# Weight matrices stored in DRAM in the order and shape in which the kernel loads them

## The chip, the cores and the metric

One core of one Trainium2 chip runs the whole program. The metric is device time in microseconds (us) of one execution, as the median of several runs. The core has TensorE (PE: matmuls, and PEld for its weight loads), VectorE (DVE), ScalarE (ACT), GpSimd (POOL) and SyncE (SP), and 16 DMA engines. SP issues all the DMAs of this kernel; the 16 engines carry them out.

## The reference, cut to what matters

Two blocks in sequence on 256 tokens of 1024 features, in float32:

```
x = first_block(...)     # modulation (w_ada), in projection (w_in), Fourier mix and
                         # neighbourhood attention, gates (w_branch_gate), out projections
                         # (w_fourier_out, w_attn_out, w_out), MLP (w_mlp1, w_mlp2)
second_block(x, ...):
  h = rms_norm_2(x);  p = h @ w_in_2                 # memory attention, conv branch,
  x = x + concat(branches) @ w_out_2                 # two-way recurrent branch
  # 16 experts, each takes its 32 best tokens of 256
  xe  = h[idx]
  hid = silu(xe @ w_gate[e]) * (xe @ w_up[e])        # each weight [1024, 1024]
  ye  = (hid @ w_down[e]) * gates
  x   = x.at[idx].add(ye);  final norm
```

The experts' weights are 16 x 3 matrices of 4 MB, 201 MB together. The other large weights are about 100 MB together.

## The kernel before

The program runs through the stages in the order above. Every weight is read once, in pieces of 1 MB (in a few places 512, 640 or 768 KB), each by one DMA of SP into a place of 128 partitions x 8 KB. The tiles are the same before and after: a piece in SBUF always holds 2048 float32 (8 KB) per partition.

- `wload` (line 273) loads a piece of the first block and of the second block's projections into one of a few places called `raw`. Its source is a view of the weight as `jax` stores it, row after row. SP issues the next load into a place as soon as the last reader of the place is done. `wsplit` (line 282) then makes two tiles `split` from it on ACT and DVE (a high and a low part), and TensorE multiplies these.
- `dense_steps` takes pieces of all 1024 rows and 256 columns (its matrices are w_in_2, w_branch_gate, w_mlp1, w_out and others): partition p gets, from each of eight groups of 128 rows, 256 columns, so eight runs of 1 KB. With 512 rows (w_fourier_out, w_attn_out) there are four runs of 2 KB.
- `tok_steps` takes pieces of 512 rows and 512 columns (w_in): four runs of 2 KB, of rows 8 KB apart in DRAM.
- `first` (w_in, columns 0 to 1023) and `down` (w_mlp2) take 256 rows: two runs of 4 KB.
- `shift_scale` takes the first third of w_ada in eight pieces of 256 columns: eight runs of 1 KB. `ada_steps` takes the other two thirds in 16 pieces of 128 rows and 2048 columns: already one run of 8 KB per partition, of rows 24 KB apart.
- `ring_load` (line 1818) issues the loads of the experts' weights into a ring of places, called `ew`; a load is issued on SP when a place comes free. The order of the pieces is fixed: for each expert four pieces of gate, four of up, four of down. Each is 256 rows of 1024 columns, so two runs of 4 KB per partition. The down matrix of the last expert is loaded by columns (`LAST`, line 32): three pieces of 256 columns (eight runs of 1 KB) and two of 128 columns (eight runs of 512 bytes).

In the expert loop TensorE multiplies the gate and up pieces into `pgu`, ACT and DVE make `hid` of it, TensorE transposes it (`phT`), multiplies the down pieces into `pd`, and adds the gated result into `acc`. The products go through the line 249, for all stages. TensorE works at one of two clocks, 2.4 GHz or 1.2 GHz; the profile shows the granted clock as a share of the higher one.

Of the kernel before, what the change touches and what calls it, by code (L numbers as in the profile page):

```python
# [31 lines left out]
LAST = (0, 256), (512, 768), (256, 384), (768, 1024), (384, 512)  # columns of the last expert's results, in order  # L32
# [97 lines left out]
# ---------------------------------------------------------------- layout of the small inputs  # L130
# [13 lines left out]
_o = 0  # L144
# [36 lines left out]

def arrays(inputs):
    out = {}
    for n in _BIG:
        a = np.ascontiguousarray(np.asarray(inputs[n]))
# [20 lines left out]
class Body:  # L206
# [7 lines left out]
    # ---- small helpers  # L214
# [47 lines left out]
    # ---- weights: loaded in pieces of 1 MB, split in halves of a piece  # L262
# [10 lines left out]
    def wload(self, src, k):  # L273
# [6 lines left out]
        return view  # L280
# [11 lines left out]
    def dense_steps(self, w, c0, c1, nk, sets, evacs, pieces=None, wide=False, preload=0, fine=False, between=None):  # L292
# [10 lines left out]
        def load(c):  # L303
            piece[c] = self.wload(w[0:nk * 128, c:c + per].rearrange("(k p) f -> p k f", p=128), nk)
# [66 lines left out]
    def tok_steps(self, w, c0, c1, sets, outs):  # L371
        """Products of [1024 features] with the tokens out on partitions: outs()[set][half], psum."""
# [5 lines left out]
        def prepare(r, h):  # L378
            if h == 0:
                piece[r] = self.wload(w[r * 128:(r + kc) * 128, c0:c1].rearrange("(k p) f -> p k f", p=128), kc)  # L380
            return self.wsplit(piece[r][:, h * kc // 2:(h + 1) * kc // 2])
# [18 lines left out]
    def in_turn(self, engines="PE DVE Activation"):  # L400
        """What follows comes after what was traced before on these engines."""
# [35 lines left out]
    def rstd(self, ps):  # L437
        """Reciprocal norms along the free axis [128, 256], the same on all partitions, from sums of squares [128, 2]."""
# [7 lines left out]
    def transpose_in(self, tok, out):  # L446
        """Two tiles [128, 1024] with the tokens on partitions to [128, 8, 256] features on partitions."""
# [58 lines left out]
    # ---- the whole  # L506
# [70 lines left out]
    def memory(self, tok, y):  # L577
        """Keys and values of the memory: steps for its norm, the keys, the values.

        tok, y: allocate two tiles [128, 1024], one [128, 16, 256]."""  # L580
# [24 lines left out]
        return (self.normed(A["mem_2"], tok, mT),  # L605
                [(None, scale)] + self.dense_steps(A["w_mk_2"], 0, 256, 8, H, [ev]),
                self.tok_steps(A["w_mv_2"], 0, 256, H, outs) + [(None, out)])

    def ada_steps(self, bank, mod, tag="pw"):
        """A third of the modulation: mod[:, r, i] for its 16 feature tiles."""  # L610
        w = self.A["w_ada"]
        acc = {}

        def prepare(k):
            return self.wload(w[k * 128:(k + 1) * 128, bank * 2048:(bank + 1) * 2048]
                              .rearrange("p (k f) -> p k f", k=4), 4)
# [39 lines left out]
    def mixers(self, x0):  # L656
        tc, nc, A, sm = self.tc, self.nc, self.A, self.sm
        w = A["w_in"]
# [26 lines left out]
        with ExitStack() as es:  # L685
# [20 lines left out]
            def shift_scale(g):  # L706
                """The first third of the modulation for the feature tiles 2 g, 2 g + 1, and their inputs."""
                bank, raws = {}, []

                def load(z):  # L710
                    c = z * 1024 + g * 256
                    raws.append(self.wload(A["w_ada"][:, c:c + 256].rearrange("(k p) f -> p k f", p=128), 8))
# [29 lines left out]
            def first():  # L742
                """Fourier features and queries, eight feature tiles side by side for inputs that come one by one."""
# [3 lines left out]
                def load(n):  # L747
                    piece[n] = self.wload(w[n * 256:(n + 1) * 256, 0:1024].rearrange("(k p) f -> p k f", p=128), 2)
# [27 lines left out]
            def weave(steps, others, n):  # L776
                """One of the others after each n of the steps."""
# [50 lines left out]
        with att as es:  # L828
# [8 lines left out]
            def norms(_):  # L837
                """Reciprocal norms of q, k and context k."""
# [31 lines left out]
            def score(i, e, j):  # L870
                """Softmax of 128 queries of a head."""
# [20 lines left out]
            def apply(i, e, j):  # L892
                """The values of the same queries."""
# [45 lines left out]
            def gating():  # L939
                for z in range(2):  # L940
# [4 lines left out]
                    yield from self.dense_steps(A["w_branch_gate"], z * 1024, (z + 1) * 1024, 8, [X], [ev_g])  # L945

            def out_fourier():
# [3 lines left out]
                return self.dense_steps(A["w_fourier_out"], 0, 1024, 4, [(yfh, yfl)], [ev])  # L951
# [28 lines left out]
    def merge_mlp(self, x0, yfh, yfl, yah, yal, gates):  # L980
        nc, A, b8 = self.nc, self.A, self.b8
        modB, modC = self.mod[1], self.mod[2]
        with ExitStack() as es:
# [41 lines left out]
            # MLP  # L1025
# [4 lines left out]
            def up(c):  # L1030
# [8 lines left out]
                return self.dense_steps(A["w_mlp1"], c * 256, (c + 1) * 256, 8, H, [ev_u], wide=c == 0)  # L1039

            def down(c):
                piece = []

                def prepare(k):
                    if k == 0:
                        piece.append(self.wload(A["w_mlp2"][c * 256:(c + 1) * 256, :]
                                                .rearrange("(k p) f -> p k f", p=128), 2))
# [18 lines left out]
            def down_last():  # L1066
                """The last three halves of pieces side by side, so that the sums end one after the other."""
# [29 lines left out]
            def steps():  # L1097
                ao = self.dense_steps(A["w_attn_out"], 0, 1024, 4, [(yah, yal)], [ev_a])
                wo = self.dense_steps(A["w_out"], 0, 1024, 8, [(mhi, mlo)], [ev_o], wide=True)
# [23 lines left out]
    def block2(self, x2):  # L1123
        """Adds the three branches to x2."""
        with ExitStack() as es:
# [5 lines left out]
            # the branches' results, (hi, lo) per feature tile  # L1131
# [23 lines left out]
    def out_proj(self, x, ob, h, between=0):  # L1155
        """Part of the rows of the out projection, added to x."""
        def ev(i, pv):
# [3 lines left out]
        return self.dense_steps(self.A["w_out_2"][a * 128:b * 128], 0, 1024, b - a, [o], [ev], preload=2, fine=not h,  # L1161
                                between=between and partial(self.ring_load, between))

    def branches(self, x2, hi, lo, ob):
        tc, nc, A, sm, rp = self.tc, self.nc, self.A, self.sm, self.rp
        w = A["w_in_2"]
        # small weights and constants
# [5 lines left out]
        def matrices(n):  # L1173
            """Room for masked scores, which serves the projections before."""
# [22 lines left out]
        # ---- projections  # L1197
# [42 lines left out]
        # ---- memory attention  # L1240
# [54 lines left out]
        def decays():  # L1295
            """Learning rates, decays and gates from the narrow projections."""
# [53 lines left out]
        def keys():  # L1350
# [5 lines left out]
            # reciprocal norms of the heads, on the rows 32 i, 32 i + 1  # L1356
# [18 lines left out]
        def start(d):  # L1375
            """Decayed keys and queries."""
# [49 lines left out]
        # ---- conv branch  # L1426
# [3 lines left out]
        def conv_pe():  # L1430
            """Taps of the last tile: products on ScalarE, summed by TensorE."""
# [43 lines left out]
        # ---- recurrent branch  # L1475
# [6 lines left out]
        # what lasts longest first  # L1482
# [11 lines left out]
        def pad(d, i):  # L1494
            """Queries of two heads, each with zeros for the other, [f, e, j, y, t]."""
# [4 lines left out]
        def scores(d, i, z):  # L1500
            """Masked scores of two heads and both chunks, [s, y, (chunk, head), t]."""
# [12 lines left out]
        def diagonal(d, i):  # L1514
            """The diagonal blocks of 16."""
# [8 lines left out]
        def values(d, i):  # L1524
            """Token-major keys of the first chunk; the values through the scores of the keys."""
# [19 lines left out]
        def first_scores(d):  # L1545
            """What the inverses need."""
# [14 lines left out]
        def blocks16(d):  # L1561
            """Inverses of the diagonal blocks of 16, rows on partitions; then as block-diagonal matrices."""
# [580 lines left out]
```

## Time and profile before

| | |
|---|---|
| time, median of 3 runs | 1208.2 us (1208.07 to 1209.84) |
| span of the profiled execution | 1205.4 us |
| what lies around that span, by the median | 2.8 us |
| busy PE / DVE / ACT | 1078.5 / 513.1 / 431.8 us |
| bytes moved by DMA | 313.89 MB, in 127687 packets |

The span runs from the first to the last instruction of the profiled execution; the runs are timed without the profiler, so the two differ. A packet is one contiguous run that a DMA engine moves. The DMA share of a stretch is the time of its packets summed over the 16 engines, over 16 times the stretch; it can pass 100% because one packet's time overlaps its neighbour's a little. GB/s is what the 16 engines moved together. A busy PE includes matmuls that are slowed by a low clock.

### The profile page before, as it was taken

The page shows a single profiled execution, that of the slowest core. Times are in us where ns is not written, and L with a number is a line of the kernel's source. Part 1 is how long each engine was busy: PE and PEld are TensorE (multiplying, and loading weights), DVE is VectorE, ACT ScalarE, POOL GpSimd, SP SyncE. Part 2 cuts the span into 40 slices and gives each one's busy share as a digit, 9 for nine tenths or more (in the row PEclk, how much of TensorE's full clock was granted, in tenths as well). Part 3 has the DMA queues.
Part 4 walks back from the last instruction along what each step waited for, and adds up shares of the span by engine and source line. Part 5 has one row for each costly group of instructions (what it writes and reads, how often), then busy time and mean ns, then how long its engine had stood idle before and what let it go on. Part 6 is the DMA issues. An engine that isn't in the chain of part 4 may idle for free.

```text
span 1205.4 us, 19234 instructions
## 1 busy us (share of the span) xinstructions
PE 1078.5 (89%) x8140; PEld 759.2 (63%) x8140; DVE 513.1 (43%) x968; ACT 431.8 (36%) x742; POOL 47.6 (4%) x53
## 2 busy tenths in 40 slices
PE   4999999999999999998899998999777777777785
PEld 3886677899999999998578786435322222222222
DVE  2554355577655555669896554212111111111102
ACT  3541367657444444575654433111000000000003
POOL 0010000011000000102210002000000000000000
PEclk8999999999999999999999998999978888888886
DMA  9874545574665563431101478999999999999997
GB/s 325 306 258 174 175 137 196 184 245 148 213 199 175 179 196 125 163 106 39 68 1 58 151 282 346 400 408 409 409 408 409 409 408 409 408 409 409 409 409 252
DMA packets 127687, 313.89 MB, mean 260 GB/s; under 512 B 6128, under 2 KB 65776, under 8 KB 125424
## 3 DMA queue, kind: packets, MB, share of 16 engines
q1 hardware_dynamic: 127600, 312.66, 70.4%
q8 instruction: 64, 1.05, 0.4%
q14 instruction: 23, 0.19, 0.0%
HBM read 311.59 MB, written 1.05 MB: 259 GB/s over the span
## 4 chain that ended last, share of the span: by engine, by line
PE 70%; DMA 20%; DVE 5%; ACT 2%; issue 1%; POOL 1%; SPq 1%; ACTq 0%; DVEq 0%
PE pw L249 23%; DMA ew<-in_w_e_up_dram 18%; PE pd L249 9%; PE acc L249 9%; PE pgu L249 5%; PE pv L249 2%; PE pada L249 2%; PE pqf L249 2%; PE py L249 1%; PE pg L249 1%; PE psc L249 1%; PE po L249 1%; DMA raw<-in_w_ada_dram 1%; PE pp L249 1%; PE psab L249 1%; DMA ew<-in_w_e_down_dram 1%
## 5 line engine op out<-in xcount | busy, mean ns | idle before, releaser
L234 DVE TENSOR_TENSOR split<-raw,split 128x1024 fp32r<-128x1024 f32 (+2 forms) x148 | 176.7, 1204 | 115.0 <-ACT split L228 114.4
L249 PE MATMUL pgu<-ew,XE 128*32 128x256 f32 x2048 | 150.9, 431 | 59.6 <-DMA ew<-in_w_e_up_dram 54.6
L228 ACT ACTIVATE split<-raw 128x1024 fp32r<-128x1024 f32 (+2 forms) x148 | 151.5, 1032 | 123.8 <-PE pw L249 63.0
L249 PE MATMUL pd<-ew,hidT 128*32 128x512 f32 (+2 forms) x560 | 159.7, 619 | 9.1 <-DVE hidT L2037 7.7
L249 PEld LDWEIGHTS pgu<-ew,XE 128*32 128x32 f32 x2048 | 64.6, 119 | 136.3 <-DMA ew<-in_w_e_up_dram 81.4
L249 PEld LDWEIGHTS pd<-ew,hidT 128*32 128x32 f32 x560 | 42.0, 120 | 116.9 <-issue 101.4
L249 PE MATMUL acc<-uh,split 128*128 128x256 f32 x512 | 94.7, 283 | 0.0
L249 PE MATMUL pw<-h2h,split 128*128 128x256 f32 x512 | 92.9, 280 | 0.0
L246 DVE SCALAR_TENSOR_TENSOR hid<-pgu,rs,hid 128x256 f32<-128x256 f32 x16 | 7.7, 484 | 197.3 <-ACT hid L225 197.3
L246 DVE SCALAR_TENSOR_TENSOR ye<-pd,ig,ye 128x512 fp32r<-128x512 f32 (+2 forms) x35 | 24.6, 705 | 151.2 <-ACT ye L225 149.6
L225 ACT ACTIVATE hid<-pgu,rs 128x256 f32<-128x256 f32 x16 | 7.6, 474 | 222.7 <-PE pgu L249 222.7
L225 ACT ACTIVATE ye<-pd,ig 128x512 fp32r<-128x512 f32 (+2 forms) x35 | 22.8, 651 | 173.6 <-PE pd L249 173.6
L249 PEld LDWEIGHTS acc<-uh,split 128*128 128x128 f32 x512 | 80.8, 192 | 0.0
L249 PEld LDWEIGHTS pw<-h2h,split 128*128 128x128 f32 x512 | 79.2, 188 | 0.0
L249 PE MATMUL acc<-ul,split 128*128 128x256 f32 x256 | 72.5, 283 | 0.0
L249 PE MATMUL pw<-h2l,split 128*128 128x256 f32 x256 | 71.4, 279 | 0.0
L249 PE MATMUL pw<-hxh,split 128*128 128x256 f32 x320 | 61.5, 286 | 0.0
L249 PE MATMUL pw<-hmh,split 128*128 128x256 f32 x320 | 61.1, 288 | 0.0
L249 PEld LDWEIGHTS pw<-hxh,split 128*128 128x128 f32 x320 | 49.9, 188 | 8.6 <-issue 4.3
L249 PEld LDWEIGHTS pw<-hmh,split 128*128 128x128 f32 x320 | 50.6, 192 | 1.6 <-PE pz L249 0.5
L249 PEld LDWEIGHTS acc<-ul,split 128*128 128x128 f32 x256 | 49.0, 191 | 0.2 <-DVE ul L234 0.2
L249 PEld LDWEIGHTS pw<-h2l,split 128*128 128x128 f32 x256 | 48.0, 187 | 0.0
(444 smaller groups left out, 1789.3 us busy)
## 6 DMA issues: line engine op xcount, KB each, us to landing
ew<-in_w_e_gate_dram SPq DMA_DIRECT2D x64, 1024.0 KB, 18.4
ew<-in_w_e_up_dram SPq DMA_DIRECT2D x64, 1024.0 KB, 18.4
ew<-in_w_e_down_dram SPq DMA_DIRECT2D x63, 1024.0 KB, 18.6
raw<-in_w_mlp_dram SPq DMA_DIRECT2D x32, 1024.0 KB, 5.5
raw<-in_w_ada_dram SPq DMA_DIRECT2D x24, 1024.0 KB, 5.9
raw<-in_w_in_dram SPq DMA_DIRECT2D x18, 1024.0 KB, 5.3
raw<-in_w_branch_gate_dram SPq DMA_DIRECT2D x8, 1024.0 KB, 5.6
raw<-in_w_out_dram SPq DMA_DIRECT2D x4, 1024.0 KB, 7.0
```

What stands on the lines that cost most here:

```text
L225: self.nc.scalar.activation(out, in_, func, **kw)
L228: self.nc.scalar.activation(out, in_, AF.Copy)
L234: self.nc.vector.tensor_tensor(out=out, in0=a, in1=b, op=op)
L246: self.nc.vector.scalar_tensor_tensor(out=out, in0=a, scalar=s, in1=b, op0=op0, op1=op1)
L249: self.nc.tensor.matmul(out, lhsT, rhs, start=start, stop=stop, **kw)
```

## The change

On the host, before the kernel runs, each large weight is stored piece by piece in the order in which the kernel loads it, and within a piece partition after partition: the 8 KB that one partition receives stand together. A piece of 1 MB is then one contiguous block of DRAM, and its DMA has one run of 8 KB per partition. The smaller pieces have runs of 4 KB (the two last ones of 512 KB), 5 KB and 6 KB (the out projection of the second block). The order of the DMAs, their number, their bytes, their destinations, the tiles and every instruction of the compute engines are the same. The pieces of `ada_steps` keep their length of run; their rows are now 8 KB apart and not 24 KB. The small inputs (tokens, constants, masks) are stored as before.

```diff
+_PIECES = {
+    "w_ada": ([(0, 1024, z * 1024 + g * 256, z * 1024 + (g + 1) * 256) for g in range(4) for z in range(2)]
+              + _by_rows(0, 1024, 128, 2048, 4096) + _by_rows(0, 1024, 128, 4096, 6144)),
+    "w_in": (_by_rows(0, 1024, 256, 0, 1024) + _by_cols(0, 1024, 1024, 1536, 256)
+             + _by_rows(0, 1024, 512, 1536, 2048)),
+    "w_branch_gate": _by_cols(0, 1024, 0, 2048, 256),
...
+    "w_mlp1": _by_cols(0, 1024, 0, 4096, 256),
+    "w_mlp2": _by_rows(0, 4096, 256, 0, 1024),
...
+    "w_e_gate_2": _by_rows(0, 16384, 256, 0, 1024),
+    "w_e_up_2": _by_rows(0, 16384, 256, 0, 1024),
+    "w_e_down_2": _by_rows(0, 15360, 256, 0, 1024) + [(15360, 16384, a, b) for a, b in LAST],
+}
...
+def _in_pieces(name, a):
+    a = np.asarray(a)
+    a = a.reshape(-1, a.shape[-1])
+    out = np.empty(a.size, a.dtype)
+    for r0, r1, c0, c1 in _PIECES[name]:
+        o, f = _PLACES[name, r0, r1, c0, c1], c1 - c0
+        out[o:o + (r1 - r0) * f] = a[r0:r1, c0:c1].reshape(-1, 128, f).transpose(1, 0, 2).reshape(-1)
+    return out
...
+    def wsrc(self, name, r0, r1, c0, c1):
+
+        o, n = _PLACES[name, r0, r1, c0, c1], (r1 - r0) * (c1 - c0)
+        return self.A[name][o:o + n].rearrange("(p f) -> p f", p=128)
+
+    def wload(self, name, r0, r1, c0, c1, k=None):
...
-        view = raw[:, 0:k * src.shape[2]].rearrange("p (k f) -> p k f", k=k)
+        src = self.wsrc(name, r0, r1, c0, c1)
+        view = raw[:, 0:src.shape[1]]
...
-            w = self.A[nm][e]
+            flat = t.rearrange("p k f -> p (k f)")
             if (nm, e) == ("w_e_down_2", 15):
                 a, b = LAST[q]
-                t = t.rearrange("p k f -> p (k f)")[:, 0:8 * (b - a)].rearrange("p (k f) -> p k f", k=8)
-                w = w[:, a:b]
+                flat = flat[:, 0:8 * (b - a)]
+                t = flat.rearrange("p (k f) -> p k f", k=8)
+                w = self.wsrc(nm, e * 1024, (e + 1) * 1024, a, b)
             else:
-                w = w[q * 256:(q + 1) * 256]
+                r = e * 1024 + q * 256
+                w = self.wsrc(nm, r, r + 256, 0, 1024)
             with self.in_turn("SP"):
-                self.nc.sync.dma_start(t, w.rearrange("(k p) f -> p k f", p=128))
+                self.nc.sync.dma_start(flat, w)
```

## Rows read from the trace of the kernel before

**Rows 1.** The page: DMA share in tenths and GB/s, 40 slices of 30 us

```profile
DMA  9874545574665563431101478999999999999997
GB/s 325 306 258 174 175 137 196 184 245 148 213 199 175 179 196 125 163 106 39 68 1 58 151 282 346 400 408 409 409 408 409 409 408 409 408 409 409 409 409 252
```

**Rows 2.** The critical chain from 770 us: start, length (us), what

```profile
774.73 6.62 PE pgu L249 x116
...
795.48 6.62 PE pgu L249 x116
...
855.72 18.46 DMA ew<-in_w_e_up_dram
...
906.24 1.98 PE pgu L249 x16
...
967.67 1.98 PE pgu L249 x16
...
1184.04 10.79 DMA ew<-in_w_e_down_dram
```

**Rows 3.** DMA in the stretch 860 to 1180 us: packets, bytes, share of 16 engines

```profile
DMA packets 33999, 130.78 MB, mean 409 GB/s; under 512 B 1994, under 2 KB 2157, under 8 KB 33982
...
q1 hardware_dynamic: 33982, 130.53, 102.3%
...
ew<-in_w_e_up_dram SPq DMA_DIRECT2D x40, 1024.0 KB, 18.6
```

**Rows 4.** DMA from 740 to 765 us, GB/s in slices of 0.6 us

```profile
GB/s 419 400 400 419 406 393 406 419 413 419 374 52 52 26 0 0 59 85 400 419 426 400 406 419 400 393 151 308 406 374 354 413 413 433 387 400 406 419 413 420
```

**Rows 5.** DMA from 17 to 21 us, where only runs of 1 KB are loaded

```profile
DMA packets 1377, 1.39 MB, mean 348 GB/s; under 512 B 16, under 2 KB 1377, under 8 KB 1377
```

**Rows 6.** DMA at 72 to 73.5 and 158 to 159.6 us: w_ada, 8 KB runs alone

```profile
DMA packets 78, 0.64 MB, mean 426 GB/s; under 512 B 0, under 2 KB 0, under 8 KB 0
...
DMA packets 84, 0.69 MB, mean 430 GB/s; under 512 B 0, under 2 KB 0, under 8 KB 0
```

**Rows 7.** DMA at 65.3 to 67 us: 4 KB runs alone, as short a stretch

```profile
DMA packets 190, 0.71 MB, mean 419 GB/s; under 512 B 16, under 2 KB 16, under 8 KB 190
```

**Rows 8.** Windows of 860 to 950 us: busy PE, PEld, DVE, ACT, POOL; clock; DMA

```profile
860.00:900.00 40.00, 29.61 (x256) 11.62 (x256) 4.74 (x11) 1.87 (x4) 0.00 (x0) 0.86 1.03 409
900.00:950.00 50.00, 38.52 (x246) 12.53 (x248) 4.11 (x9) 2.32 (x4) 0.00 (x0) 0.74 1.02 409
```

**Rows 9.** Timeline of PE at the end: start, length, what [idle before, its releaser]

```profile
1188.46 3.66 PE L249 MATMUL pd<-ew,hidT 128*32 128x256 f32 x32 [0.52 <-DVE hidT L2037]
...
1194.97 1.07 PE L249 MATMUL pd<-ew,hidT 128*32 128x256 f32 x16 [0.78 <-DMA ew<-in_w_e_down_dram]
```

**Rows 10.** Timeline of PE at the start, the same columns

```profile
20.59 1.07 PE L249 MATMUL pada<-raw,cs 128*32 128x256 f32 x16 [1.65 <-DVE hxl L234]
23.48 1.94 PE L249 MATMUL pada<-raw,cs 128*32 128x256 f32 x16 [1.82 <-DMA raw<-in_w_ada_dram]
```

**Rows 11.** Windows at the start, columns as in rows 8

```profile
20.00:22.00 2.00, 1.07 (x16) 0.50 (x16) 1.44 (x4) 2.00 (x4) 0.00 (x0) 0.91 1.10 357
22.00:24.00 2.00, 0.52 (x8) 0.29 (x12) 1.87 (x2) 0.42 (x1) 0.00 (x0) 0.50 1.04 404
...
28.00:30.00 2.00, 2.00 (x18) 2.00 (x16) 0.00 (x0) 0.00 (x0) 0.00 (x0) 0.88 1.10 350
```

**Rows 12.** Critical chain, 60 to 720 us: its only DMA

```profile
131.08 5.37 DMA raw<-in_w_branch_gate_dram
```

**Rows 13.** DMA issues from 104 to 112 us: a w_ada load, us to landing

```profile
raw<-in_w_ada_dram SPq DMA_DIRECT2D x1, 1024.0 KB, 4.8
```

**Rows 14.** Waits of 60 to 240 us that end with a DMA: us, times, longest

```profile
ACT split L228 <- DMA raw<-in_w_branch_gate_dram: 7.9, 3, 3.3
...
ACT split L228 <- DMA raw<-in_w_in_dram: 1.1, 1, 1.1
```

**Rows 15.** DMA at 91 to 92.6 and 222.5 to 225 us: 2 KB runs

```profile
DMA packets 297, 0.61 MB, mean 379 GB/s; under 512 B 1, under 2 KB 1, under 8 KB 297
...
DMA packets 512, 1.02 MB, mean 406 GB/s; under 512 B 16, under 2 KB 16, under 8 KB 512
```

More of the change, by code (lines that the diff above doesn't have):

```diff
@@ L179, with _by_rows, _by_cols @@
         "iclr_up_2", "gate_up_2", "w_out_2", "w_router_2", "w_e_gate_2", "w_e_up_2", "w_e_down_2"]
+def _by_rows(r0, r1, n, c0, c1):
+    return [(r, r + n, c0, c1) for r in range(r0, r1, n)]
+def _by_cols(r0, r1, c0, c1, n):
+    return [(r0, r1, c, c + n) for c in range(c0, c1, n)]
+_PIECES = {
[4 more added lines that the diff above has]
+    "w_branch_gate": _by_cols(0, 1024, 0, 2048, 256),
+    "w_fourier_out": _by_cols(0, 512, 0, 1024, 512),
+    "w_attn_out": _by_cols(0, 512, 0, 1024, 512),
+    "w_out": _by_cols(0, 1024, 0, 1024, 256),
+    "w_mlp1": _by_cols(0, 1024, 0, 4096, 256),
+    "w_mlp2": _by_rows(0, 4096, 256, 0, 1024),
+    "w_mk_2": [(0, 1024, 0, 256)],
+    "w_mv_2": [(0, 1024, 0, 256)],
+    "w_in_2": _by_cols(0, 1024, 0, 2560, 256),
+    "w_out_2": _by_cols(0, 640, 0, 1024, 256) + _by_cols(640, 1024, 0, 1024, 512),
+    "w_e_gate_2": _by_rows(0, 16384, 256, 0, 1024),
+    "w_e_up_2": _by_rows(0, 16384, 256, 0, 1024),
+    "w_e_down_2": _by_rows(0, 15360, 256, 0, 1024) + [(15360, 16384, a, b) for a, b in LAST],
+}
+_PLACES = {}
+for _n, _l in _PIECES.items():
+    _o = 0
+    for _p in _l:
+        _PLACES[(_n, *_p)] = _o
+        _o += (_p[1] - _p[0]) * (_p[3] - _p[2])
+def _in_pieces(name, a):
[6 more added lines that the diff above has]
+    return out
 def arrays(inputs):
@@ L184, in arrays @@
     for n in _BIG:
+        if n in _PIECES:
+            out[n] = _in_pieces(n, inputs[n])
+            continue
         a = np.ascontiguousarray(np.asarray(inputs[n]))
@@ L290, in wsplit, with dense_steps @@
         return hi, lo
-    def dense_steps(self, w, c0, c1, nk, sets, evacs, pieces=None, wide=False, preload=0, fine=False, between=None):
+    def dense_steps(self, w, c0, c1, nk, sets, evacs, pieces=None, wide=False, preload=0, fine=False, between=None,
+                    r0=0):
         half = {3: 256, 5: 128}.get(nk) or 1024 // nk
@@ L303, in load @@
         def load(c):
-            piece[c] = self.wload(w[0:nk * 128, c:c + per].rearrange("(k p) f -> p k f", p=128), nk)
+            piece[c] = self.wload(w, r0, r0 + nk * 128, c, c + per)
         def prepare(c, h):
@@ L379, in prepare @@
             if h == 0:
-                piece[r] = self.wload(w[r * 128:(r + kc) * 128, c0:c1].rearrange("(k p) f -> p k f", p=128), kc)
+                piece[r] = self.wload(w, r * 128, (r + kc) * 128, c0, c1)
             return self.wsplit(piece[r][:, h * kc // 2:(h + 1) * kc // 2])
@@ L605, in memory @@
         return (self.normed(A["mem_2"], tok, mT),
-                [(None, scale)] + self.dense_steps(A["w_mk_2"], 0, 256, 8, H, [ev]),
-                self.tok_steps(A["w_mv_2"], 0, 256, H, outs) + [(None, out)])
+                [(None, scale)] + self.dense_steps("w_mk_2", 0, 256, 8, H, [ev]),
+                self.tok_steps("w_mv_2", 0, 256, H, outs) + [(None, out)])
     def ada_steps(self, bank, mod, tag="pw"):
-        w = self.A["w_ada"]
         acc = {}
         def prepare(k):
-            return self.wload(w[k * 128:(k + 1) * 128, bank * 2048:(bank + 1) * 2048]
-                              .rearrange("p (k f) -> p k f", k=4), 4)
+            return self.wload("w_ada", k * 128, (k + 1) * 128, bank * 2048, (bank + 1) * 2048, 4)
         def compute(k, raw):
@@ L657, in mixers @@
         tc, nc, A, sm = self.tc, self.nc, self.A, self.sm
-        w = A["w_in"]
+        w = "w_in"
         both = self.b1.tile([128, 16, 256], F32, tag="y", name="xncn", bufs=1)
@@ L711, in load @@
                     c = z * 1024 + g * 256
-                    raws.append(self.wload(A["w_ada"][:, c:c + 256].rearrange("(k p) f -> p k f", p=128), 8))
+                    raws.append(self.wload("w_ada", 0, 1024, c, c + 256))
                 def products(z):
@@ L747, in load @@
                 def load(n):
-                    piece[n] = self.wload(w[n * 256:(n + 1) * 256, 0:1024].rearrange("(k p) f -> p k f", p=128), 2)
+                    piece[n] = self.wload(w, n * 256, (n + 1) * 256, 0, 1024)
                 def split(k):
@@ L944, in ev_g @@
                         self.act(gates[z][:, i:i + 2], pv, AF.Sigmoid)
-                    yield from self.dense_steps(A["w_branch_gate"], z * 1024, (z + 1) * 1024, 8, [X], [ev_g])
+                    yield from self.dense_steps("w_branch_gate", z * 1024, (z + 1) * 1024, 8, [X], [ev_g])
             def out_fourier():
@@ L950, in ev @@
                     self.tt(g[:, i:i + 2], g[:, i:i + 2], pv, ALU.mult)
-                return self.dense_steps(A["w_fourier_out"], 0, 1024, 4, [(yfh, yfl)], [ev])
+                return self.dense_steps("w_fourier_out", 0, 1024, 4, [(yfh, yfl)], [ev])
             units = [(i, e, j) for i in range(4) for e in range(2) for j in range(2)]
@@ L1038, in ev_u @@
                     self.put_split(uh, ul, r)
-                return self.dense_steps(A["w_mlp1"], c * 256, (c + 1) * 256, 8, H, [ev_u], wide=c == 0)
+                return self.dense_steps("w_mlp1", c * 256, (c + 1) * 256, 8, H, [ev_u], wide=c == 0)
             def down(c):
@@ L1160, in out_proj @@
         o = tuple(Tiles(lambda k, z=z: ob[a + k][:, z]) for z in range(2))
-        return self.dense_steps(self.A["w_out_2"][a * 128:b * 128], 0, 1024, b - a, [o], [ev], preload=2, fine=not h,
-                                between=between and partial(self.ring_load, between))
+        return self.dense_steps("w_out_2", 0, 1024, b - a, [o], [ev], preload=2, fine=not h,
+                                between=between and partial(self.ring_load, between), r0=a * 128)
     def branches(self, x2, hi, lo, ob):
         tc, nc, A, sm, rp = self.tc, self.nc, self.A, self.sm, self.rp
-        w = A["w_in_2"]
+        w = "w_in_2"
         heads = rp.tile([128, 416], F32, name="heads")
```

10 lines of the change are left out of this document (4 added, 6 removed).

## The prediction, before the result was known

> **What bounds the kernel now.** I read the page's slices first: the DMA rate stands at 408 to 409 GB/s, flat, from slice 27 to slice 39, and far below it in the middle of the kernel [rows 1]. A flat ceiling over 13 slices, with the share of the DMA engines in the highest tenth, is what a transfer bound looks like. The chain of waits says from when it decides. Until 841 us an expert follows the one before in 20.7 us (774.73 to 795.48) and the chain holds TensorE alone; from 855 us each round holds a wait of some 18 to 22 us for an up piece, and two rounds take 61.4 us (906.24 to 967.67), 30.7 us per expert [rows 2]. An expert is 12 pieces of 1 MB, 12.58 MB; at 409 GB/s that is 30.8 us, the same number. So TensorE can do an expert in 20.7 us and gets one in 30.7 us. The windows agree: with 409 GB/s, TensorE is busy 30 of 40 us, part of them at the lower clock (granted share 0.74 to 0.86), so it has room [rows 8]. A piece needs 18.6 us from issue to landing [rows 3], which at 409 GB/s is seven pieces in the queue: the DMA engines never wait for an issue there.
>
> From when is the queue full? At 746 to 751 us the rate falls to zero once, because no place of the ring is free; from 751 us it stays [rows 4]. Between 751 and 855 us TensorE sets the chain, but it works off pieces that have landed and frees places faster (12.58 MB in 20.7 us, 608 GB/s) than the engines fill them. The stream therefore runs without a break from 751 us to the landing of the last up piece at 1184.04 us [rows 2, 4]: 433 us whose length is bytes over rate.
>
> In the rest DMA stands on the chain in two places: a load of w_ada at the start, for which TensorE sits idle 1.82 us [rows 10], and one load of w_branch_gate at 131 us [rows 12]. In the MLP and in the second block the pieces arrive before TensorE wants them.
>
> **The change, part by part.** No instruction of a compute engine is added or removed, and the bytes are the same. What changes is the number of packets: a 1 MB piece of an expert has 128 and not 256, a piece of `dense_steps` 128 and not 1024. So the question is what a packet costs beside its bytes.
>
> *The stream of experts.* Runs of 1 KB, with the queue full, come at 348 GB/s [rows 5], runs of 4 KB at 409 [rows 3]. Per engine that is 16 x 1.024/348 = 47.1 ns and 16 x 4.096/409 = 160.2 ns a packet: 37.7 ns for each KB and 9.4 ns for the packet. By that line a packet of 8 KB takes 311 ns, or 421.5 GB/s. The trace holds runs of 8 KB too, in the loads of w_ada: in two short stretches with nothing else they came at 426 and 430 GB/s [rows 6]. Short stretches flatter: 4 KB runs reach 419 in one [rows 7] where the long stream has 409. I take the line. 433 us x (1 - 409/421.5) = **12.8 us**. Bounds: from stretch to stretch (419 to 428) the gain is 2.1%, 9.1 us; if the long stream reached the 430 of the best stretch, 433 x (1 - 409/430) = 21.1 us; if it keeps 409, nothing.
>
> *The end.* The last down matrix comes in runs of 1 KB and 512 B. In the profile 4 MB of it need 10.79 us after the last up piece [rows 2]; at 421 GB/s they need 10.0 us, and the smaller packets' cost that is saved belongs to the part ahead too. But TensorE begins on them only at 1188.46 and waits for one of them 0.78 us [rows 9]. All other steps from the last up piece to the end are products, gates and the norm. So the end gives **0.8 us**, bounds 0 and 0.8.
>
> *The start.* The awaited w_ada load is the fourth of its kind, behind one w_in piece and behind the tokens. Four pieces at 348 GB/s take 3.01 us each, at 421.5 GB/s 2.49: 2.1 us sooner, and the w_in piece a little. That covers the wait of 1.82 us. TensorE's clock is at half there: it fell within 20 to 22 us, about when the product before the wait ended, and came back shortly after 28 us [rows 10, 11]. If that stretch keeps its place, work done earlier in it runs at half speed and the 1.82 us bring **0.9 us**. Bounds: nothing (another wait takes its place: DVE's `split`, which must end first) and 1.8 us (the clock does not fall).
>
> *The load at 131 us.* It is alone in the queue, 5.37 us from issue to landing [rows 12]. A lone load with 8 KB runs takes 4.8 us [rows 13]. ACT waits for it at the end, so **0.4 us** of the 0.6 pass on; ACT's two other waits of its kind [rows 14] are off the chain. Bounds 0 and 1.0, should the others count.
>
> *SP's issues* are as many and in the same order; SP waits for places, not for its own work. I cost this at nothing. Where loads are hidden (MLP, second block) they land sooner and TensorE does not see it; nothing hangs on that cover, since landing sooner uncovers no work.
>
> Sum: 12.8 + 0.8 + 0.9 + 0.4 = 14.9 us. The profiled execution has a span of 1205.4 us, so the new span is 1190.5; the runs' median is 2.8 us above the span, and I carry that over: 1208.2 - 14.9 = **1193.3 us**, a ratio of 0.988.
>
> **The rivals.**
>
> *The packet's own cost is smaller in a long stream than the line says.* For: the shortest stretches differ less, 419 against 426 GB/s [rows 6, 7], or 1.6%. Against: over several us 1 KB runs lie 15% under 4 KB runs, which needs a cost of about 9 ns for each packet. The stage then gives 433 x 0.016 = 7.1 us, and with the 2.1 us of the other parts the time is 1199.0.
> The Trainium skill, page "DMA: Bandwidth & Descriptors", section "Why small descriptors are slow (HBM only)", gives a packet a fixed overhead of about 3 cycles beside one per 32 bytes; by that a run of 8 KB costs 259 cycles for twice 131, an estimate of 1.1% or 5.0 us for the stage, and 1201.1 us in all. The trace speaks against so small a price: by the same rule 1 KB runs would lie 6% under 4 KB runs, and they lie 15% under [rows 3, 5].
>
> *Nothing in the long stream.* Something other than the packets sets 409 GB/s (the memory, the way into SBUF), or the 8 KB are moved as two packets again. For: the rate is very flat [rows 1], and flatter than in the short stretches. Against: w_ada's rows show packets of 8 KB above 420 [rows 6]. Then only 2.1 us are left: 1206.1, within the measurement.
>
> *Slower: the new addresses collide.* In step, the 16 engines now read blocks whose partitions lie 8 KB apart, all pieces alike. For: one load whose rows lie 8 KB apart, of 2 KB runs, came at 379 GB/s, where 2 KB runs at 4 KB distance came at 406 [rows 15]; the stretch is short and includes a start. Against: the expert pieces of before are read at distances that are powers of two as well (4 KB), at 409. If the stream fell to 379, the stage would take 433 x (409/379 - 1) = 34 us more: 1240. It decides from below 407 GB/s on, where the stage loses what the other parts bring.
> [...]
>
> *The stream reaches the rate of the best stretch*, 430 GB/s [rows 6]: 21.1 + 2.1 us, 1185.0.
>
> **How the numbers follow.** Chances: forecast 0.72 (its own range 1188 to 1198); smaller packet cost 0.08; nothing in the stream 0.07; slower 0.06; best rate 0.07. The range of 8 in 10 takes in the smaller packet cost on one side and half of the best rate on the other: 1186 to 1202. About 0.2%, 2.4 us, is what a measurement can tell from no change here. Forecast, smaller cost and best rate are faster by more: 0.87; nothing in the stream, 2.1 us, counts as the same: 0.07; the collision is slower: 0.06.
>
> **What would show it.** In the profile after: packets of the main queue fall to less than half, with most of 8 KB; the flat part of the DMA row stands near 421 GB/s; two experts take 59.7 us and not 61.4; the chain still has the up pieces, a little shorter. At the end TensorE no longer waits for a down piece; at the start the 1.82 us before `pada` are gone; loads that were 1 KB runs show up to 420 GB/s. Wrong would be: a flat part at 409 with packets of 8 KB (the bytes are the limit), a rate with dips (collisions), or a flat part at 421 with gaps in which the engines wait for a free place, since then the ring and not the rate would set the length.

## The result, and the profile after

The changed kernel takes 1191.6 us (median of 4 runs, 1191.05 to 1192.07), before 1208.2 (1208.07 to 1209.84): a ratio of 0.9865, with an interval of 0.9851 to 0.9879. It is faster by 16.7 us; predicted were 14.9. Its profiled execution has a span of 1189.8 us against 1205.4, which is 15.6 us less. In all runs of this case that have both on record the time lies 1.7 to 1.9 us above the span. The 2.8 us of before therefore say that its profile is of an execution about 1 us shorter than the median: the stretches below can show 15.6 of the 16.7 us.

The page of the changed kernel, answering to [rows 1]: DMA share and GB/s in 40 slices, all packets, and the main queue.

```profile
DMA  9774545464555543521101368899999999999996
GB/s 357 291 275 155 177 155 194 182 240 146 212 195 191 177 178 111 207 108 36 72 1 46 142 269 358 355 419 420 418 421 418 420 419 418 420 419 421 418 420 273
DMA packets 46919, 313.89 MB, mean 264 GB/s; under 512 B 6128, under 2 KB 6896, under 8 KB 10480
...
q1 hardware_dynamic: 46832, 312.66, 66.6%
```

The bytes are those of before, the packets 46919 instead of 127687, and the flat part of the rate stands at 418 to 421 GB/s.

DMA of the changed kernel from 860 to 1160 us, answering to [rows 3], with the time from issue to landing as the last number:

```profile
DMA packets 17260, 125.80 MB, mean 419 GB/s; under 512 B 1918, under 2 KB 1918, under 8 KB 1918
...
q1 hardware_dynamic: 17244, 125.56, 101.0%
...
ew<-in_w_e_up_dram SPq DMA_DIRECT2D x40, 1024.0 KB, 19.9
```

All but the 1918 small packets now have 8 KB. The engines are as full as before and move 2.5% more. The chain of the changed kernel, answering to [rows 2] (start, length, work):

```profile
899.30 1.98 PE pgu L299 x16
...
919.26 19.92 DMA ew<-in_w_e_down_dram
...
939.24 19.88 DMA ew<-in_w_e_up_dram
...
959.19 19.89 DMA ew<-in_w_e_gate_dram
...
1080.37 1.98 PE pgu L299 x16
...
1160.22 19.11 DMA ew<-in_w_e_down_dram
```

The stretch is still bound by transfers. From 899.30 to 1080.37 us six experts pass, 60.4 us for two. New is that a transfer on the chain often follows a transfer, with no product between them; the last section says why.

To place the gain I cut each span at three points that every kernel has: the first product into `pss`, the first into `pxe` (the tokens of an expert, ahead of the stream; its start on the chain), and the start of the last product with an up piece (the last group of `pgu`). In us:

| profile | to `pss` | to `pxe` | to the last up product | to the end | GB/s, 860 to 1160 us |
|---|---|---|---|---|---|
| before | 57.6 | 687.9 | 438.7 | 21.2 | 409 |
| changed | 54.6 | 687.6 | 428.4 | 19.2 | 419 |
| difference | -3.0 | -0.3 | -10.3 | -2.0 | |

### The profile page after: what moved, and what is told of

Its sections match the earlier page's. It is cut to its first block, busy times and chain, and to the rows that moved or that the text cites. A ratio compares the mean times of both kernels' runs of the same rounds, so it can differ in the third digit from the quotient of the medians.

```text
span 1189.8 us, 19234 instructions
## 1 busy us (share of the span) xinstructions
PE 1074.5 (90%) x8140; PEld 758.5 (64%) x8140; DVE 513.0 (43%) x968; ACT 431.9 (36%) x742; POOL 47.6 (4%) x53
## 2 busy tenths in 40 slices
DMA packets 46919, 313.89 MB, mean 264 GB/s; under 512 B 6128, under 2 KB 6896, under 8 KB 10480
## 4 chain that ended last, share of the span: by engine, by line
PE 62%; DMA 31%; DVE 2%; ACT 2%; POOL 1%; issue 1%; SPq 0%; ACTq 0%
PE pw L299 23%; DMA ew<-in_w_e_down_dram 12%; DMA ew<-in_w_e_up_dram 11%; PE acc L299 8%; DMA ew<-in_w_e_gate_dram 7%; PE pd L299 4%; PE pada L299 2%; PE pv L299 2%; PE psab L299 2%; PE pqf L299 2%; PE pgu L299 2%; PE py L299 1%; PE pg L299 1%; PE psc L299 1%; PE po L299 1%; DMA raw<-in_w_ada_dram 1%
## 5 line engine op out<-in xcount | busy, mean ns | idle before, releaser
L299 PE MATMUL pd<-ew,hidT 128*32 128x512 f32 (+2 forms) x560 | 156.9, 603 | 9.5 <-DVE hidT L2093 7.8
## 6 DMA issues: line engine op xcount, KB each, us to landing
ew<-in_w_e_gate_dram SPq DMA_DIRECT2D x64, 1024.0 KB, 19.9
ew<-in_w_e_up_dram SPq DMA_DIRECT2D x64, 1024.0 KB, 19.9
ew<-in_w_e_down_dram SPq DMA_DIRECT2D x63, 1024.0 KB, 19.9
```

Source lines behind the costliest of these rows:

```text
L299: self.nc.tensor.matmul(out, lhsT, rhs, start=start, stop=stop, **kw)
```

## The experiments

Each kernel is the changed one with the edit shown. Times are medians; ratios are to the kernel before on the same chip, with their 95% intervals. The stretches are those of the table above and come from one execution each; that of all but experts is the longest of its five (1204.9 us), so its stretches show 2.4 of the 5.1 us that the median gives.

| run | us | ratio | to `pss` | to `pxe` | to last up | end | GB/s |
|---|---|---|---|---|---|---|---|
| experts only | 1195.1 | 0.9884 to 0.9914 | 58.2 | 688.1 | 427.0 | 19.7 | 419 |
| all but experts | 1202.4 | 0.9945 to 0.9973 | 57.2 | 687.2 | 437.4 | 21.2 | 409 |
| w_ada only | 1207.1 | 0.9984 to 1.0002 | 56.3 | 687.8 | 438.7 | 22.9 | 409 |
| w_ada and w_in only | 1205.0 | 0.9967 to 0.9985 | 55.4 | 688.2 | 438.4 | 21.2 | 409 |
| the others only | 1206.2 | 0.9974 to 0.9993 | 57.3 | 687.7 | 438.6 | 21.2 | 409 |
| experts, 8 KB runs 32 KB apart | 1192.7 | 0.9864 to 0.9894 | 54.8 | 689.4 | 428.1 | 19.1 | 419 |
| experts, 2 KB runs | 1228.7 | 1.0158 to 1.0188 | 54.9 | 687.4 | 463.8 | 20.3 | 386 |
| experts, 1 KB runs (one run) | 1276.1 | | 54.7 | 687.3 | 512.6 | 19.9 | 348 |
| last matrix in short runs | 1194.7 | 0.9872 to 0.9904 | 56.3 | 687.9 | 427.4 | 21.1 | 419 |
| experts, two pieces by a load | 1196.9 | 0.9899 to 0.9926 | 54.6 | 687.7 | 433.2 | 19.8 | 424 |
| changed, once more | 1189.9 | 0.9841 to 0.9880 | 54.2 | 687.2 | 427.2 | 19.2 | 419 |

**Halves of the change.** A weight that stays as it was stored is sent unchanged and read by rows:

```diff
+        if _plain(name):
+            return self.A[name][r0:r1, c0:c1].rearrange("(k p) f -> p k f", p=128)
```

`_plain` is true for all but the experts' weights (first run), for those alone (second), for all but w_ada (third).

> Only the experts' three weights are stored in pieces; all other weights as in the kernel before. Theory, that each packet costs some 8 to 9 ns of an engine's time beside its bytes: the stream of experts runs at 419 GB/s as in the changed kernel and is 10.0 us shorter, the end is 2.2 us shorter, the start is as before: 1208.2 - 12.2 = 1196.0 us, packets of the main queue about 79000. Rival, that the first part's shorter loads feed the stream (an earlier start of it is where the time comes from): 1203 us or more, and 409 GB/s.

> The reverse of the run before: all weights but the experts' are stored in pieces. Theory: the stream stays at 409 GB/s and only starts sooner, by 3.3 us, of which 2.9 us arise before 30 us: 1204.9 us. Rival, that the gain outside the stream is the one wait of 1.82 us and the load at 131 us as forecast (0.9 + 0.4 us): 1206.9 us. A sum of this gain and that of the experts alone that lies well off 16.7 us would mean that the two parts work on each other.

> Only w_ada is stored in pieces. Theory, that TensorE waits at the start twice for loads of w_ada (at 20.59 us too, where the profile names DVE): the third load's product begins at about 18.8 us and not at 20.6, the fourth at 21.2 and not 23.5, and the time falls by 2.9 us to 1205.3 us. Rival, that the first of the two waits was DVE's hxl as the profile names it, and went away for another reason (the w_in pieces, SP's blocked issues): the third product still begins at 20.6 us and the time is 1207 us.

The experts alone bring 12.4 us (1207.5 to 1195.1), the rest 5.1: together 17.5, about what the whole brings (16.7, and 17.5 in its second measurement). The halves add up, and the rest gave more than the 3.3 us expected of it. The third run missed: 0.4 us, with an interval that holds no change, where 2.9 were expected. Its timeline of PE shows why (start, length, work, idle time before and what ended it):

```profile
19.32 1.07 PE L307 MATMUL pada<-raw,cs 128*32 128x256 f32 x16
...
21.30 1.07 PE L307 MATMUL pada<-raw,cs 128*32 128x256 f32 x16 [0.91 <-DMA raw<-in_w_ada_dram]
...
41.66 1.07 PE L307 MATMUL pada<-raw,cs 128*32 128x256 f32 x16 [2.11 <-DMA raw<-in_w_ada_dram]
```

The first products came about as early as expected (19.32 and 21.30, expected 18.8 and 21.2), but a later load of w_ada, in a queue with w_in pieces that are still stored by rows, kept TensorE waiting 2.11 us at 41.66. The end of this execution took 22.9 us, its last products at the lower clock. So two more runs part the rest in two:

> w_ada and w_in are stored in pieces, nothing else. With w_ada alone the time fell by 0.4 us (not told from nothing), with all weights but the experts' by 5.1. Theory, that the start needs both, since pieces of both stand in the same queue and a faster w_ada only moves the wait to a later piece behind a w_in piece (at 41 us TensorE waited 2.1 us for a w_ada load in that run): 3 to 5 us less than the kernel before, 1202.5 to 1204.5 us beside its 1207.5. Rival, that the start gives nothing and the others of the first part do it: within 1 us of the kernel before.

> The complement: the weights of the gates, of the out projections, of the MLP and of the second block are stored in pieces; w_ada, w_in and the experts' as before. Theory: only the load of w_branch_gate at 131 us stood on the chain, so 0.3 to 0.5 us less than the kernel before, which is inside the interval: ratio 0.9990 to 1.0000. Rival, that these weights hold the rest of the 5.1 us: 1203 to 1205 us.

w_ada with w_in gives 2.8 us, a little under the 3 to 5 expected, and the others 1.5 by the medians and 2.0 by the ratio, more than the 0.3 to 0.5 expected. So the start needs w_in beside w_ada; that w_in pieces ahead in the queue are the reason is argued and not shown. The profile of the others shows only 0.3 us at the start and 0.2 in the middle; about 1 us of it has no place in the trace and stays open.

**Where the runs lie.** The first run below spreads a piece's 8 KB runs over an expert's matrix, 32 KB apart:

```diff
+    if name.startswith("w_e_"):
+        m = (15 if name == "w_e_down_2" else 16) * 1024 * 1024
+        out[:m] = out[:m].reshape(-1, 4, 128, 2048).transpose(0, 2, 1, 3).reshape(-1)
...
```

The second keeps a piece as one block of 1 MB, but stores it as 4 blocks of [128, 512], so that a partition gets four runs of 2 KB; a third does the same with 8, runs of 1 KB:

```diff
+def _runs(name, r0, r1, c0, c1):
+    return 4 if name.startswith("w_e_") and r1 - r0 == 256 else 1
...
+        x = a[r0:r1, c0:c1].reshape(-1, 128, f).transpose(1, 0, 2).reshape(128, n, -1)
+        out[o:o + (r1 - r0) * f] = x.transpose(1, 0, 2).reshape(-1)
```

> The changed kernel, but the four pieces of each expert's matrix are interleaved in DRAM: still one run of 8 KB per partition, but the runs of one piece lie 32 KB apart and not 8 KB, and no piece is one block. Theory, that the number of packets alone counts: no change from the changed kernel, 1191.6 us, 419 GB/s, the same packets. Rival, that the contiguous block of 1 MB or the distance of the runs sets the rate: between 1193 and 1208 us, with the flat part between 409 and 418 GB/s.

> The changed kernel, but each full piece of the experts' weights is stored as four blocks of 128 x 2 KB: the piece is still one contiguous block of 1 MB, loaded in the same order, with four runs of 2 KB per partition. Theory, a fixed cost per packet: from 4 KB (409 GB/s, 160.2 ns of an engine a packet) and 8 KB (419, 312.8 ns) follow 7.6 ns for the packet and 38.15 ns for each KB, so 83.9 ns for 2 KB and 391 GB/s; the stream of 177 MB takes 453 us and not 423: about 1222 us. With the forecast's line (9.4 ns and 37.7 ns) it would be 386 GB/s and 1227 us. Rival, that the contiguous block is what counts: 419 GB/s and 1192 us.

> As the run with 2 KB, with eight blocks of 128 x 1 KB per piece. Runs of 2 KB came at 386 GB/s, 84.9 ns a packet. Theory, a fixed cost per packet: 47.1 ns and 348 GB/s as in the stretch of w_ada loads at the start of the kernel before; the stream of 177 MB takes 508 us, the time is about 1277 us. Rival, that the low rate at the start came from the distance of w_ada's rows or from the start itself: over 360 GB/s and under 1260 us.

DMA from 860 to 1160 us, in this order: runs 32 KB apart, 2 KB runs, 1 KB runs.

```profile
DMA packets 17256, 125.80 MB, mean 419 GB/s; under 512 B 1914, under 2 KB 1914, under 8 KB 1914
```

```profile
DMA packets 58272, 115.91 MB, mean 386 GB/s; under 512 B 1770, under 2 KB 1770, under 8 KB 58258
...
ew<-in_w_e_up_dram SPq DMA_DIRECT2D x39, 1024.0 KB, 14.4
```

```profile
DMA packets 103205, 104.25 MB, mean 348 GB/s; under 512 B 1588, under 2 KB 103191, under 8 KB 103191
...
ew<-in_w_e_gate_dram SPq DMA_DIRECT2D x36, 1024.0 KB, 11.9
```

8 KB runs out of four interleaved pieces come at the same 419 GB/s. One solid block of 1 MB, in runs of 2 KB, comes at 386, below the 409 of before. So it is neither the block nor, at 8 KB and 32 KB, the distance of the runs; it is their length. The times follow the prediction's line: 2 KB took 1228.7 us where the line gave 1227 (and the later one, from 4 and 8 KB, 1222), 1 KB 1276.1 where 1277 was expected.

**The last matrix** in eight runs per partition again, all else as changed: `_runs` gives 8 for the pieces of `LAST` and 1 elsewhere.

> The changed kernel, but the five pieces of the last expert's down matrix keep their short runs: eight runs of 1 KB (of 512 bytes in the two halves) per partition. Theory, that the end is bound by these loads: the last lands 10.8 us after the last up piece and not 8.7, and the time is 2.0 us above the changed kernel's, 1193.6 us. Forecast's view, that TensorE's own work sets the end but for 0.78 us: 0.8 us above at most, 1192.4 us.

By time this run decides nothing: 0.9872 to 0.9904 overlaps the changed kernel's interval. Its profile, with those of the others, does decide; the section after this one reads them.

**Longer runs than the change has.** Places of 16 KB per partition, each loaded with two pieces by one DMA; single pieces keep 8 KB runs.

```diff
-        self.ring_room(RING0)
+        self.ring_room(RING0, 4)
...
-                w = self.wsrc(nm, r, r + 256, 0, 1024)
+                w = self.A[nm][e * 1048576 + q // 2 * 524288:][:524288].rearrange("(p f) -> p f", p=128)
```

> The changed kernel with 14 of the ring's 21 places joined to seven places of 16 KB per partition: where such a place is free, two pieces that follow each other are loaded by one DMA with one run of 16 KB per partition. Theory, a cost of 7.6 to 9.4 ns for each packet: a packet of 16 KB takes some 618 ns of an engine, 424 GB/s; with two thirds of the pieces in pairs the flat part stands at 422 to 423 GB/s and the time is 3 to 4 us under the changed kernel's on the same chip. Rival, that 419 GB/s is a ceiling of another kind (runs of 8 KB came at 426 and 430 in short stretches but never for long): 419 GB/s and no gain. Second rival: places that come free only after two pieces make the engines wait, and the time is above the changed kernel's.

> The changed kernel once more, beside the run with pairs on one chip: 1191 to 1193 us, ratio to the kernel before 0.985 to 0.988.

DMA from 860 to 1160 us with pairs:

```profile
DMA packets 11329, 127.32 MB, mean 424 GB/s; under 512 B 1253, under 2 KB 1253, under 8 KB 1253
...
q1 hardware_dynamic: 11313, 127.08, 100.5%
```

DMA from 742 to 790 us in slices of 1.2 us, with pairs and then in the changed kernel's second measurement (1189.9 us, a little under the 1191 to 1193 expected):

```profile
GB/s 423 410 416 82 7 0 232 314 437 437 396 259 396 410 410 423 437 437 437 437 423 437 423 246 14 0 14 130 266 430 430 416 485 437 437 423 437 423 437 437
```

```profile
GB/s 41 27 55 266 423 314 348 369 335 410 410 444 403 423 416 437 423 437 410 423 403 430 423 423 423 423 403 416 410 430 423 416 416 410 423 423 430 430 410 423
```

The rate rose as the cost of a packet says: the 10060 packets that are not small carry what 15513 packets of 8 KB would, so some 5450 of them have 16 KB, seven tenths of the bytes. But a place of 16 KB comes free only when two pieces are used, and the engines stood idle a second time, near 772 us, where the changed kernel has no gap. The stretch takes 6.0 us more than in the changed kernel run beside it (433.2 against 427.2), and the time is 7 us longer. Counted in bytes, 2.2 MB less had been loaded when the stretch begins, which is some 5 us; by 40 us later another 2.2 MB are missing, the gap's 5 us; and the better rate gives 4.6 us of it back. A better rate lost to a later start.

## Why the prediction was right, and where its terms were off

**The bound and the mechanism held.** A full queue, a flat rate, a length that is bytes over rate: where the rate changed, the stretch to the last up product followed (512.6 us at 348 GB/s, 463.8 at 386, 438.7 at 409, 428.4 at 419), and the stretch ahead of it kept its 687.2 to 688.2 us in all but one profile. Engine time per packet, 16 x size/rate, is 47.1 ns for 1 KB, 84.9 for 2, 160.2 for 4 and 312.8 for 8 KB. A line through the two shortest (37.8 ns for each KB, 9.3 for the packet) gives 160.5 and 311.7 for the two longer: what the prediction drew from a stretch of 4 us [rows 5] and the long stream [rows 3] held over the whole range. The records of the single packets say the same: from 860 to 1160 us a packet of 1, 2, 4, 8 and 16 KB took 51.2, 88.3, 163.7, 315.1 and 617.6 ns in the mean, close to 37.7 ns for each KB and 13 for the packet. (Neighbours overlap a little, so these lie above the times from the rate.)

The Trainium skill, page "DMA: Bandwidth & Descriptors", section "Why small descriptors are slow (HBM only)", prices a packet at about 3 cycles beside one per 32 bytes, by estimate 0.09 KB's worth. The runs show 9.3 ns beside 37.8 ns for a KB, 0.25 KB's worth, so the measurement disagrees with the page, and that rival (1199 to 1201 us) is out. For the rival of colliding addresses the same page of the Trainium skill, section "Latency and other measured facts", lists copies with rows from 512 KiB (207 GB/s) to 4 MiB and 8 MiB apart (103 GB/s), where 214 is full rate; here 8 KB and 32 KB apart gave the same 419 GB/s, and no run reached such a distance.

| term, us | predicted | measured in the two profiles | over all profiles |
|---|---|---|---|
| stream | 12.8 | 10.3 | |
| end | 0.8 | 2.0 | 1.9 |
| start | 0.9 | 3.0 | 2.5 |
| load at 131 us | 0.4 | 0.3 (the whole middle) | |
| sum | 14.9 | 15.6 | |

The last column is the mean of the profiles with the old layout less that with the new: at the end six (21.1 to 22.9) and seven (19.1 to 20.3), at the start three (57.3 to 58.2) and nine (54.2 to 57.2, w_ada and w_in both new). The sum came close partly by luck: a term too large met two too small, and both of these lie outside the bounds that the prediction gave them (0 to 0.8 for the end, 0 to 1.8 for the start).

**The stream** was sized 2.5 us too large. Its step "421.5 GB/s" became 419: 433 x (1 - 409/419) = 10.3 us. A packet of 8 KB took 312.8 ns and not 311; two experts took 60.4 us and not 59.7. One premise was wrong without harm: "SP waits for places, not for its own work". The last section shows that SP was inside its issues for 282 of 300 us, and no place held it up; the engines were full all the same.

**The start** was the step that failed most in proportion. The prediction counted only the wait of 1.82 us [rows 10] and took the one ahead of it, named there as a wait for DVE's `hxl`, as given. PE's timeline of the changed kernel, answering to [rows 10]:

```profile
18.83 1.07 PE L299 MATMUL pada<-raw,cs 128*32 128x256 f32 x16
...
21.23 1.80 PE L299 MATMUL pada<-raw,cs 128*32 128x256 f32 x16 [1.33 <-DMA raw<-in_w_ada_dram]
```

and DVE's:

```profile
19.93 0.89 DVE L284 TENSOR_TENSOR hxl<-h,hxh 128x256 fp32r<-128x256 f32 x2
```

The product begins 1.76 us sooner than its 20.59, and ahead of `hxl`: it never needed `hxl`. With the experts alone changed, the old loads give that wait its right name:

```profile
20.74 1.07 PE L307 MATMUL pada<-raw,cs 128*32 128x256 f32 x16 [1.12 <-DMA raw<-in_w_ada_dram]
```

So TensorE waited for two loads, and both came sooner. The chain has the second of them from its issue to its landing, before and in the changed kernel:

```profile
9.49 13.94 DMA raw<-in_w_ada_dram
```

```profile
6.11 15.08 DMA raw<-in_w_ada_dram
```

It landed at 21.19 us and not at 23.43, 2.2 us sooner, much as the prediction's 2.1 us for four pieces said. It was issued sooner too, but the engines' share from 5 to 20 us was 92% or more in both kernels, so the rate set the landing. What failed is the step from there: the prediction let 1.82 us of the 2.1 count, and half of that. The second wait was to vanish and did not (1.33 us left), because its product was wanted earlier too. The windows, answering to [rows 11] (PE, PEld, DVE, ACT, POOL, clock, DMA share, GB/s):

```profile
20.00:22.00 2.00, 0.77 (x12) 0.43 (x16) 1.44 (x4) 2.00 (x3) 0.00 (x0) 0.86 1.02 422
22.00:24.00 2.00, 2.00 (x17) 1.19 (x10) 1.70 (x2) 0.85 (x2) 0.00 (x0) 0.50 1.03 426
24.00:26.00 2.00, 2.00 (x15) 2.00 (x15) 0.00 (x0) 0.00 (x0) 0.00 (x0) 0.79 0.75 229
```

The loads come at 422 to 426 GB/s, and the lower clock (1.2 GHz) ends within 24 to 26 us, where before it reached past 28: the assumption that the slow stretch "keeps its place" did not hold either. On the chain the awaited product begins 2.25 us sooner (23.48 to 21.23), takes 0.14 us less, and the next products take 3.86 us instead of 4.41: 2.94 us together. The second measurement of the changed kernel stood at the higher clock throughout the start and was only 0.4 us ahead there (54.2 against 54.6), so most of the gain is from the loads.

**The end.** The prediction let the loads give no more than TensorE's wait of 0.78 us. PE's timeline of the changed kernel, answering to [rows 9]:

```profile
1170.63 1.58 PE L299 MATMUL pgu<-ew,XE 128*32 128x256 f32 x16 [0.56 <-DMA ew<-in_w_e_up_dram]
...
1175.72 1.07 PE L299 MATMUL pd<-ew,hidT 128*32 128x256 f32 x16 [0.36 <-DMA ew<-in_w_e_down_dram]
...
1179.47 1.07 PE L299 MATMUL pd<-ew,hidT 128*32 128x256 f32 x16 [0.77 <-DMA ew<-in_w_e_down_dram]
```

The same view of the run with only w_ada and w_in changed (short last loads), and of the one with only the experts changed (long ones):

```profile
1181.96 1.58 PE L307 MATMUL pgu<-ew,XE 128*32 128x256 f32 x16 [0.64 <-DMA ew<-in_w_e_up_dram]
...
1187.97 1.07 PE L307 MATMUL pd<-ew,hidT 128*32 128x256 f32 x16 [1.27 <-DMA ew<-in_w_e_down_dram]
...
1192.76 1.07 PE L307 MATMUL pd<-ew,hidT 128*32 128x256 f32 x16 [1.69 <-DMA ew<-in_w_e_down_dram]
```

```profile
1173.22 1.93 PE L307 MATMUL pgu<-ew,XE 128*32 128x256 f32 x16 [0.57 <-DMA ew<-in_w_e_up_dram]
...
1177.47 3.21 PE L307 MATMUL pd<-ew,hidT 128*32 128x256 f32 x32 [0.52 <-DVE hidT L2102]
...
1182.54 1.07 PE L307 MATMUL pd<-ew,hidT 128*32 128x256 f32 x16
```

Count from the last up product to the third `pd` product of 256 columns, the last that may wait for a load. With short loads it begins 10.8 us later (1194.97 less 1184.20 before, 1192.76 less 1181.96 here), whether two products ahead of it take 3.66 us together [rows 9] or 1.07 each: the loads set it. With long loads it begins 8.84 us later where TensorE's products are short (changed, a load still sets it) and 9.32 where they are long (experts only, and no wait for a load). So the loads came 2.0 us sooner, and how much of it counts depends on TensorE's clock in that execution. In the profile of before the clock was at its lower level until about 1192 us, and TensorE would have been ready for that product only 0.78 us sooner; it is ready sooner still in the run of the experts only, where 1.5 us count, and in the changed kernel, at the higher clock from 1173 us, where all 2.0 do. The wait of 0.78 us was thus the smallest of its kind: with the same short loads TensorE waits 1.27 and 1.69 us in the run with w_ada and w_in. That step of the prediction, the loads give what TensorE's wait shows, is the one that failed.

The prediction's sum for these loads has a slip as well. The load of 10.79 us [rows 2] is the fourth of five, and with it 3.67 MB of the matrix had landed and not all 4.19: at 421.5 GB/s these need 8.7 us and not 10.0, which is what the changed kernel shows.

The wait that was to go is still there, 0.77 us, because TensorE is ready sooner. In the run with the last matrix alone in short runs that product begins 10.7 us later with no wait: TensorE stood at the lower clock so long that it was free at 1182.32 us, just as the load landed (1182.27). So the time of that run does not tell what the loads are worth, but its landing does: 10.65 us after the last up piece, as before (10.67), where long runs take 8.75.

**The load at 131 us** is off the chain, as predicted in size. ACT's waits for loads of w_branch_gate from 60 to 240 us, answering to [rows 14]:

```profile
ACT split L278 <- DMA raw<-in_w_branch_gate_dram: 6.7, 3, 2.9
```

**What would have shown it wrong** did not appear in the changed kernel: no dips, no 409 with 8 KB packets, no gap after 755 us. The gaps came with places of 16 KB only. Of its other signs two did not come: TensorE's waits at the start and at the end are still there.

## What to carry to other kernels

Where a chain of waits is bound by transfers at a flat rate, fit engine time per packet against size from stretches with a full queue; two sizes in the trace of before told the rate of a third to within 0.6%. Storing weights in the order and shape in which they are loaded adds no work on the chip, and here each doubling of the run gave less: 348, 386, 409, 419 GB/s for 1, 2, 4 and 8 KB; runs of 16 KB were not worth places that come free later. For a stall named after one releaser, ask whether the instruction needs it, and count the waits of the same kind next to it: here the wait put down to DVE was one for a load. And a wait read in one profile has its size from that execution's clock: the loads behind 0.78 us were worth 2.0.

## What the runs showed of the hardware that was not expected

How long SP is held by an issue, and so how many loads are on the way, depends on their packets. What SP waited for between its issues in the changed kernel from 860 to 1160 us (us in all, times, longest):

```profile
SPq L1886 <- DMA ew<-in_w_e_up_dram: 86.7, 40, 3.2
...
SPq L1886 <- PE pd L299: 1.0, 4, 0.3
```

How long one issue took SP there (least, median and most, in ns), in the changed kernel, before, with 2 KB and with 1 KB runs:

```profile
L1886 SPq DMA_DIRECT2D ew<-in_w_e_up_dram x40: 327/328/328, 870.8 to 1150.3; - x40
```

```profile
L1830 SPq DMA_DIRECT2D ew<-in_w_e_up_dram x37: 417/2310/4767, 878.6 to 1158.2; - x37
```

```profile
L1892 SPq DMA_DIRECT2D ew<-in_w_e_up_dram x39: 1067/2534/4579, 858.6 to 1157.6; - x39
```

```profile
L1892 SPq DMA_DIRECT2D ew<-in_w_e_up_dram x32: 2567/2872/3332, 871.7 to 1134.2; - x32
```

In the changed kernel SP issues in 0.33 us and then waits for a landing. The trace tells for which: the program's loads use eight semaphores in turn, and each load is issued after the landing of the load eight before it, 0.06 us after in the median. So it is the program that allows eight loads on the way: 19.9 us from issue to landing x 419 GB/s = 8.3 MB, eight loads of 1 MB. With pairs the next issue follows the eighth landing in the same way. That is why the chain after runs from transfer to transfer.

With shorter runs SP is inside its issues nearly all the time: 282 of the 300 us before, 291 with 2 KB and with 1 KB. The loads on the way are fewer, 14.4 us x 386 GB/s = 5.6 MB with 512 runs in each and 11.9 x 348 = 4.1 MB with 1024. It is no place that SP lacks. At 906.24 us in the kernel before TensorE takes up the piece that has just landed [rows 2], at 906.26 SP begins to issue the one eight pieces on, and the ring has 21 places. What ends so long an issue no run here shows. It cost nothing here, as the main queue kept the engines at 100% to 109% in all these runs.

The start took 54.2 to 57.2 us with one layout of its loads. The chains of the two extremes, the changed kernel's second measurement and all but experts, both at the higher clock there, differ in the load of the tokens, whose layout the change leaves alone, and in a later load of w_ada:

```profile
2.12 4.63 DMA xt<-in_x_dram
...
31.50 8.03 DMA raw<-in_w_ada_dram
```

```profile
2.12 5.90 DMA xt<-in_x_dram
...
33.29 9.22 DMA raw<-in_w_ada_dram
```

The tokens landed 1.3 us apart (6.75 and 8.02), the awaited w_ada piece 3.0 us apart. What delays the first load of an execution no run here shows. It limits what single profiles say of the start.
